# First layer of a two-layer encoder on one core: convolution taps, low halves of weights and the order of the output projection

## The chip, the cores and the metric

The kernel runs on one core of a Trainium2 chip, in one launch. The core has five engines that work side by side, each through its own instructions in order: TensorE (PE; its weight loads, PEld, overlap its matmuls), VectorE (DVE), ScalarE (ACT), GpSimd (POOL) and SyncE (SP, which here issues the DMAs). They wait for each other through semaphores. The metric is the device time of one execution in microseconds (us). The kernel before has a median of 2307.87 us over three runs (2307.01 to 2309.32).

## The reference

The input is 1024 positions by 1024 features, in float32. Layer 0 mixes a convolution branch with a gated branch; layer 1 is differential attention; a squared-ReLU MLP follows each. The change lies in layer 0's mixer, and in how the weights of layer 1 are made ready. Cut to what matters:

```python
def conv_gmlp_mixer(h, w_in, conv_w, conv_b, conv_ln_g, conv_ln_b,
                    sg_ln_g, sg_ln_b, sg_w, sg_b, w_out):
    z = h @ w_in                              # 1024 -> 512 value, 512 gate, 1024 for gMLP
    a = z[..., :512] * sigmoid(z[..., 512:1024])
    a = depthwise_conv(a, conv_w, width=31, centred) + conv_b
    a = silu(layernorm(a, conv_ln_g, conv_ln_b))
    zs = gelu(z[..., 1024:])
    u = zs[..., :512]
    v = layernorm(zs[..., 512:], sg_ln_g, sg_ln_b)
    v = einsum('gpq,bnqgc->bnpgc', sg_w, v.reshape(B, 8, 128, 4, 128)) + sg_b
    return concatenate([a, u * v], axis=-1) @ w_out

# per layer: x = x + gate * mixer(modulate(rmsnorm(x), shift, scale))
#            x = x + gate' * (relu(h' @ w1) ** 2 @ w2),  h' = modulate(rmsnorm(x), ...)
# (shift, scale, gate) = split(silu(c) @ mod_w + mod_b, 3)
```

## The kernel before

**Matmuls.** Activations lie with features on the partitions, in tiles of 128 by 512 positions (two column halves, `c` = 0 and 1). A float32 product is made of three matmuls in a faster format: each operand is split into a high half, rounded to that format, and a low half, the remainder. `mm3` issues high·high (L130), high·low (L131) and low·high (L132).

**Weights.** `prep` (L105 to L114) loads a 128x1024 piece into `raw` (SP issues the load), ScalarE casts it to `whi` (L112), and VectorE subtracts to give `wlo` (L113); in attention the subtraction is POOL's (`eng`). `raw`, `whi` and `wlo` rotate over three buffers each. 61 weights go this way: 4 stripes `wg` and 4 pieces `wa` for the gated linear unit, 8 stripes `wv` for the gMLP values (the four are loaded once for each `c`), 4 pieces `wa` for `u`, 9 pieces of `wo` for layer 0's output projection, then 24 of `wqkv` and 8 of `wo` in layer 1. The MLP weights have a path of their own and are not touched.

**Layer 0 in the order of the code.** The gated linear unit fills four padded tiles `ap`, one for each 128 channels. The values `vg` (gelu, eight tiles of 128 positions by 512) follow, and their LayerNorm is applied by VectorE (L504, `tensor_scalar` with mean and 1/deviation). For each of four groups, `u` is projected, then `gating` multiplies `vg` by the position weights (L522, 128x128 matmuls), VectorE scales and shifts the result into `tt` (L525) and multiplies it into `u` (L529); the first three groups gate after the third `u`, the last after the fourth. `split` makes the pair `zh` (ScalarE, L254) and `zl` (VectorE, L255) for the projection.

**The convolution** runs meanwhile, channel tile by channel tile (`i` = 0 to 3). 20 of 31 taps are VectorE's, summed in PSUM (`ca`, one buffer; L593, L595). For the other 11, ScalarE makes the products (the first one straight into `a1`, L587; the others into `pr`, two buffers, L590) and POOL adds them to `a1` (L591, ten adds for each channel tile). L596 adds `ca` and `a1` into a third tile, `a0`. The names in the trace are `a` for `a0` and `a1`.

**The convolution's LayerNorm** runs for each column half over the four channel tiles: matmuls with ones give the mean (L607), VectorE subtracts it (L611), ScalarE squares (L613), matmuls give the variance (L614), `rstd_of` makes 1/deviation (L198 and L207 to L213), VectorE multiplies (L625), ScalarE takes the sigmoid (L627), VectorE applies gain and bias (L628) and multiplies by the sigmoid (L630), and `split` makes `zh` and `zl`.

**The output projection** has two halves: `project_half(1, c, i)` uses the gated branch, `project_half(0, c, i)` the convolution branch. Each adds `gate` times its result to `x` (`upd`, L278). The modulation vectors (shift, scale, gate) come from `mod_unit`: a load of 512 KB into `mraw` (two buffers) and a multiply with sum on VectorE (L147). `queue_mod` queues them; `bg` and `tick` let them out.

**What sets the order.** A scheduler orders the instructions on each engine from the order of the code, buffers and dependencies; `high_priority` puts the LayerNorm statistics ahead. Pools rotate: "mm" has six PSUM banks, "cv" six tiles of 128x1024.

Of the kernel before, what the change touches and what calls it, by code (L numbers as in the profile page):

```python
# [10 lines left out]
F32 = mybir.dt.float32  # L11
# [7 lines left out]
P = 128  # L19
# [11 lines left out]
SUB_EPS = 1e-5  # L31
TAPS = 31
PAD = TAPS // 2
DVE_TAPS = 20
B_BUFS = 8

V_MIXG, V_MLPG, V_FING = 0, 16, 32
# [10 lines left out]
def trunk(ctx: ExitStack, tc: tile.TileContext, t_in, out):  # L48
# [3 lines left out]
    def f32(ap):  # L52
        return ap.bitcast(F32)
# [53 lines left out]
    def prep(src, own=None, eng=None):  # L107
        raw = wp.tile([P, D], F32, name="raw", tag="raw", bufs=3)
        load(raw, src)
        hi = (own or wp).tile([P, D], F32R, name="whi", tag="whi", bufs=1 if own else 3)  # L110
        lo = (own or wp).tile([P, D], F32R, name="wlo", tag="wlo", bufs=1 if own else 3)
        act.copy(out=hi, in_=raw)  # L112
        (eng or dve).tensor_tensor(out=lo, in0=raw, in1=f32(hi), op=ALU.subtract)  # L113
        return hi, lo  # L114

    class Stream:
# [55 lines left out]
    def vcol(v):  # L172
        return vec[:, v:v + 1]
# [173 lines left out]
    with opened(name="mix", bufs=1) as mp, ExitStack() as pst:  # L347
# [152 lines left out]
        dve.tensor_tensor(out=vt, in0=vr, in1=vr, op=ALU.mult)  # L500
        dve.tensor_tensor(out=vt, in0=vt, in1=vv, op=ALU.mult)
        dve.scalar_tensor_tensor(out=vr, in0=vt, scalar=1.5, in1=vr, op0=ALU.add, op1=ALU.mult)
        for t in range(8):
            dve.tensor_scalar(out=vg[t], in0=vg[t], scalar1=mv[:, t, 0:1], scalar2=vr[:, t:t + 1],  # L504
                              op0=ALU.subtract, op1=ALU.mult)


        ps = bank()
# [56 lines left out]
        def project_half(half, c, i):  # L565
            w = wu.get(4 + 4 * (1 - half) + i)
            for m in (2 * (i % 4), 2 * (i % 4) + 1):
# [6 lines left out]
                if half == 0:  # L574
                    nrm.add(c, x[m][c])


        acc = []
        for i in range(4):
            a = padded[i]  # L580
            a0 = mp.tile([P, T], F32, name="a0", tag="cv", bufs=6)
            a1 = mp.tile([P, T], F32, name="a1", tag="cv", bufs=6)

            def cw(w):
                return vcol(V_CW + w * 4 + i)

            act.activation(out=a1, in_=a[:, DVE_TAPS:DVE_TAPS + T], func=AF.Copy, scale=cw(DVE_TAPS))  # L587
            for w in range(DVE_TAPS + 1, TAPS):
                pr = mp.tile([P, T], F32, name="pr", tag="pr", bufs=2)
                act.activation(out=pr, in_=a[:, w:w + T], func=AF.Copy, scale=cw(w))  # L590
                conv_end = pool.tensor_tensor(out=a1, in0=a1, in1=pr, op=ALU.add)  # L591
            ca = cvps.tile([P, T], F32, name="ca", tag="ca")
            dve.tensor_scalar(out=ca, in0=a[:, 0:T], scalar1=cw(0), scalar2=vcol(V_CB + i), op0=ALU.mult, op1=ALU.add)  # L593
            for w in range(1, DVE_TAPS):
                dve.scalar_tensor_tensor(out=ca, in0=a[:, w:w + T], scalar=cw(w), in1=ca, op0=ALU.mult, op1=ALU.add)  # L595
            dve.tensor_tensor(out=a0, in0=ca, in1=a1, op=ALU.add)  # L596
            acc.append(a0)

        rs = []
        for c in range(NC):
# [10 lines left out]
                    act.activation(out=sq, in_=y, func=AF.Square)  # L613
                    last = pe.matmul(pvar, ones, sq, start=i == 0, stop=i == 3)  # L614
            rs.append(rstd_of(pvar, 512, eps_l, after=last if c == 0 else None))
        queue_mod(0, [16])
        bg(100)
        queue_mod(1, [8, 0], conv_end)
        queue_mod(1, [16])
        bg(18)  # L620
        for c in range(NC):
            cs = slice(c * C, (c + 1) * C)
            for i in range(4):
# [1 line left out]
                dve.tensor_tensor(out=y, in0=y, in1=rs[c], op=ALU.mult)  # L625
                sg = tmp.tile([P, C], F32, name="sg", tag="ht", bufs=3)
                act.activation(out=sg, in_=y, func=AF.Sigmoid, scale=vcol(V_CLG + i), bias=vcol(V_CLB + i))  # L627
                dve.tensor_scalar(out=y, in0=y, scalar1=vcol(V_CLG + i), scalar2=vcol(V_CLB + i),  # L628
                                  op0=ALU.mult, op1=ALU.add)
                dve.tensor_tensor(out=y, in0=y, in1=sg, op=ALU.mult)  # L630
                z[i][c] = htile()
                split(*z[i][c], y)
        for i in range(4):
            for c in range(NC):
                project_half(1, c, i)

        h = [[None] * NC for _ in range(KT)]
        for c, seq in ((0, (0, 1, 2, 3)), (1, (3, 2, 1, 4))):
# [575 lines left out]
```

## Time and profile before

| what | value |
|---|---|
| median of three runs | 2307.87 us (2307.01 to 2309.32) |
| the profiled execution's own time | 2309.78 us |
| its span in the trace | 2308.0 us |
| its mean granted TensorE clock | 0.982 |
| ScalarE busy | 1175.9 us (51%) |
| POOL busy | 205.3 us (9%) |
| DMA, mean over the span | 145 GB/s |

Each row of a group gives the line in the kernel, the engine, the operation, output and input by their names, shapes and count; then busy us and the mean ns of one; then the engine's idle time just before such instructions, with what ended it. A row of the timeline gives the start, the duration and the instruction, and in brackets the idle time before it and what released it. A row of the windows gives the stretch, its length, busy us and instructions of PE, PEld, DVE, ACT and POOL, then the granted TensorE clock, the DMA share and GB/s. Layer 0's mixer takes roughly the first 350 us.

### The profile page before, as it was taken

To read this page: it belongs to the slowest core of one execution; us is meant where nothing else is said; L and a number is where in the kernel's file an instruction comes from. 1 tells how busy PE (TensorE), PEld (TensorE's weight loads), DVE (VectorE), ACT (ScalarE), POOL (GpSimd) and SP (SyncE) were. 2 spreads that over 40 slices of the span, in tenths; PEclk is the share of its full clock that TensorE was granted. 3 is DMA by queue.
4 is the path that set the end of the run, shared out by engine and by line. 5 is a ranking of instruction groups with operands and counts; after the bars stand their busy time and mean duration, and the time that the engine had idled before them with its cause. 6 is when DMAs were issued, how large, how long until landed. Compare 5 with 4: busy or idle time off the path is not lost. (4 is left out here: it accounts for less than half of the span.)

```text
span 2308.0 us, 27492 instructions
## 1 busy us (share of the span) xinstructions
PE 2193.2 (95%) x10144; PEld 1802.1 (78%) x10144; DVE 1872.2 (81%) x2599; ACT 1175.9 (51%) x1745; POOL 205.3 (9%) x109
## 2 busy tenths in 40 slices
PE   4997599999999999989999999999999999999997
PEld 3786387778888888868888888887778888888886
DVE  8899899997795976987878888876699659578497
ACT  4554246643534535445666666654366354353455
POOL 0484000000000000001111111110000000000002
PEclk9998799999999999999999999999999999999999
DMA  8221553837547267234545333361352461643712
GB/s 320 83 74 46 191 159 136 326 110 275 190 155 280 102 223 261 87 110 98 100 86 109 77 84 72 81 202 51 116 228 107 163 229 47 211 144 110 246 46 74
DMA packets 113863, 335.17 MB, mean 145 GB/s; under 512 B 20576, under 2 KB 23520, under 8 KB 112704
## 3 DMA queue, kind: packets, MB, share of 16 engines
q1 hardware_dynamic: 113728, 333.41, 44.7%
q8 instruction: 80, 1.31, 0.2%
q14 instruction: 55, 0.45, 0.1%
HBM read 279.79 MB, written 53.58 MB: 144 GB/s over the span
## 5 line engine op out<-in xcount | busy, mean ns | idle before, releaser
L131 PE MATMUL ps<-b,whi 128*128 128x512 f32 (+1 forms) x1808 | 701.3, 389 | 5.6 <-DVE b L255 5.6
L130 PE MATMUL ps<-b,whi 128*128 128x512 f32 (+1 forms) x1808 | 693.7, 390 | 5.8 <-ACT b L254 3.9
L132 PE MATMUL ps<-b,wlo 128*128 128x512 f32 (+1 forms) x1808 | 693.9, 389 | 1.6 <-DVE wlo L255 1.6
L254 ACT CAST whi<-raw 128x1024 fp32r<-128x1024 f32 (+1 forms) x225 | 236.5, 1051 | 355.1 <-PE ps L131 317.3
L130 PEld LDWEIGHTS ps<-b,whi 128*128 128x128 f32 x1808 | 341.3, 189 | 78.9 <-ACT b L254 5.1
L131 PEld LDWEIGHTS ps<-b,whi 128*128 128x128 f32 x1808 | 341.1, 189 | 77.9 <-DVE b L255 7.5
L132 PEld LDWEIGHTS ps<-b,wlo 128*128 128x128 f32 x1808 | 340.9, 189 | 72.1 <-DVE wlo L255 2.1
L255 DVE TENSOR_TENSOR wlo<-raw,whi 128x1024 fp32r<-128x1024 f32 (+1 forms) x225 | 274.1, 1218 | 139.4 <-ACT whi L254 137.2
L130 PE MATMUL ps<-hh,whi 128*128 128x512 f32 x576 | 225.7, 405 | 32.7 <-ACT hh L249 15.7
L131 PE MATMUL ps<-hl,whi 128*128 128x512 f32 x576 | 229.8, 399 | 6.6 <-DVE hl L250 6.6
L132 PE MATMUL ps<-hh,wlo 128*128 128x512 f32 x576 | 228.4, 397 | 0.0
L743 DVE SCALAR_TENSOR_TENSOR x<-ps,mod,x 128x512 f32<-128x512 f32 x220 | 159.8, 746 | 41.5 <-PE ps L132 41.1
L962 ACT ACTIVATE L<-L,mn 128x1024 f32<-128x1024 f32 x128 | 147.1, 1150 | 90.8 <-DVE mn L960 89.4
L960 DVE CUSTOM_DVE_ANT_0 L<-S,B 128x1024 f32<-128x1024 f32 x128 | 156.0, 1223 | 34.7 <-PE pt L982 17.4
L113 POOL TENSOR_TENSOR wlo<-raw,whi 128x1024 fp32r<-128x1024 f32 x24 | 64.4, 2683 | 1181.6 <-PE S L957 808.4
L130 PEld LDWEIGHTS ps<-hh,whi 128*128 128x128 f32 x576 | 110.1, 192 | 60.9 <-ACT hh L249 20.1
L254 ACT CAST b<-f 128x512 fp32r<-128x512 f32 x192 | 118.0, 619 | 76.5 <-PE ps L132 74.8
L255 DVE TENSOR_TENSOR b<-f,b 128x512 fp32r<-128x512 f32 x192 | 128.9, 684 | 10.2 <-ACT b L254 10.2
L131 PEld LDWEIGHTS ps<-hl,whi 128*128 128x128 f32 x576 | 110.6, 192 | 32.7 <-DVE hl L250 10.1
L132 PEld LDWEIGHTS ps<-hh,wlo 128*128 128x128 f32 x576 | 110.4, 192 | 24.1 <-issue 0.5
L147 DVE CUSTOM_DVE_ANT_0 mraw<-mraw,cact 128x1024 f32<-128x1024 f32 x96 | 116.2, 1218 | 6.9 <-DMA mraw<-in_modw 6.8
L732 ACT COPY f<-ps 128x512 f32<-128x512 f32 x96 | 56.1, 588 | 126.8 <-PE ps L132 126.7
(195 smaller groups left out, 3463.6 us busy)
## 6 DMA issues: line engine op xcount, KB each, us to landing
b<-tspl SPq DMA_DIRECT2D x168, 512.0 KB, 5.3
raw<-in_wm SPq DMA_DIRECT2D x128, 512.0 KB, 4.6
mraw<-in_modw SPq DMA_DIRECT2D x96, 512.0 KB, 4.5
tspl<-b SPq DMA_DIRECT2D x56, 512.0 KB, 4.3
raw<-in_wqkv SPq DMA_DIRECT2D x24, 512.0 KB, 4.8
raw<-in_wo SPq DMA_DIRECT2D x17, 512.0 KB, 3.5
x<-in_xT SPq DMA_DIRECT2D x32, 256.0 KB, 5.8
tsr<-tsp SPq DMA_DIRECT2D x8, 1024.0 KB, 7.7
```

The lines of the kernel that those rows point to most:

```text
L113: (eng or dve).tensor_tensor(out=lo, in0=raw, in1=f32(hi), op=ALU.subtract)
L130: pe.matmul(ps, wh, ah, start=first, stop=False, skip_group_check=resumed)
L131: pe.matmul(ps, wh, al, start=False, stop=False, skip_group_check=resumed)
L132: newest[0] = pe.matmul(ps, wl, ah, start=False, stop=last, skip_group_check=resumed)
L147: i = dve.tensor_tensor_reduce(out=raw, in0=raw, in1=cact, op0=ALU.mult, op1=ALU.add, scale=1.0, scalar=0.0, accum_out=acc)
L254: act.copy(out=out_h, in_=src)
L255: (lo_eng or dve).tensor_tensor(out=out_l, in0=src, in1=f32(out_h), op=ALU.subtract)
L732: act.copy(out={"X1": c11, "Y1": c22, "X2": c12}[p], in_=ps)
L743: dve.scalar_tensor_tensor(out=x[m][c], in0=ps, scalar=gate(d, m), in1=x[m][c], op0=ALU.mult, op1=ALU.add)
L960: dve.tensor_tensor_reduce(out=L, in0=S, in1=win, op0=ALU.add, op1=ALU.min, scale=1.0, scalar=3e38, accum_out=mn)
L962: act.activation(out=L, in_=L, func=AF.Exp, bias=mn, scale=-1.0, accum_out=s[:, j:j + 1])
```

## The change

1. `DVE_TAPS` goes from 20 to 18: 13 taps are ScalarE's and POOL's, 12 adds for each channel tile.
2. In `prep`, the low half is made by ScalarE writing −`whi` into `wlo`, and a DMA on POOL's queue that reads the weight from DRAM once more and adds it into `wlo`. This holds for all 61 weights, so VectorE's 37 and POOL's 24 subtractions go.
3. The LayerNorm of `vg` is applied by ScalarE (scale and bias per position), with one more small VectorE operation for the bias.
4. The gated half of the output projection, with the modulation units it needs, stands ahead of the convolution in the code, and its loops run over `i` first.
5. The sum of `ca` and `a1` goes back into `a1`; `a0` is dropped.
6. Gain and bias of the convolution's LayerNorm are applied by ScalarE.
7. `bg(18)` stands after that LayerNorm's loop.

```diff
-DVE_TAPS = 20
+DVE_TAPS = 18
...
         act.copy(out=hi, in_=raw)
-        (eng or dve).tensor_tensor(out=lo, in0=raw, in1=f32(hi), op=ALU.subtract)
+        act.activation(out=lo, in_=f32(hi), func=AF.Copy, scale=-1.0)
+        pool.dma_start(out=lo, in_=src, accum_op=ALU.add)
         return hi, lo
...
         dve.scalar_tensor_tensor(out=vr, in0=vt, scalar=1.5, in1=vr, op0=ALU.add, op1=ALU.mult)
+        dve.scalar_tensor_tensor(out=vt, in0=mv[:, :, 0], scalar=-1.0, in1=vr, op0=ALU.mult, op1=ALU.mult)
         for t in range(8):
-            dve.tensor_scalar(out=vg[t], in0=vg[t], scalar1=mv[:, t, 0:1], scalar2=vr[:, t:t + 1],
-                              op0=ALU.subtract, op1=ALU.mult)
+            act.activation(out=vg[t], in_=vg[t], func=AF.Identity, scale=vr[:, t:t + 1], bias=vt[:, t:t + 1])
...
+        queue_mod(0, [16])
+        bg(100)
+        for i in range(4):
+            for c in range(NC):
+                project_half(1, c, i)
         acc = []
         for i in range(4):
             a = padded[i]
-            a0 = mp.tile([P, T], F32, name="a0", tag="cv", bufs=6)
             a1 = mp.tile([P, T], F32, name="a1", tag="cv", bufs=6)
...
-            dve.tensor_tensor(out=a0, in0=ca, in1=a1, op=ALU.add)
-            acc.append(a0)
+            dve.tensor_tensor(out=a1, in0=ca, in1=a1, op=ALU.add)
+            acc.append(a1)
...
             rs.append(rstd_of(pvar, 512, eps_l, after=last if c == 0 else None))
-        queue_mod(0, [16])
-        bg(100)
         queue_mod(1, [8, 0], conv_end)
         queue_mod(1, [16])
-        bg(18)
         for c in range(NC):
...
-                dve.tensor_scalar(out=y, in0=y, scalar1=vcol(V_CLG + i), scalar2=vcol(V_CLB + i),
-                                  op0=ALU.mult, op1=ALU.add)
+                act.activation(out=y, in_=y, func=AF.Identity, scale=vcol(V_CLG + i), bias=vcol(V_CLB + i))
                 dve.tensor_tensor(out=y, in0=y, in1=sg, op=ALU.mult)
                 z[i][c] = htile()
                 split(*z[i][c], y)
-        for i in range(4):
-            for c in range(NC):
-                project_half(1, c, i)
+        bg(18)
```

Three places show how the instructions move. Lines after the change are numbered a little higher (L591 is L597, L607 is L612, L614 is L619, L596 is L602, L525 is L526).

POOL's order before, from its first add to attention (`a_1614`, `a_1669`, `a_1724`, `a_1779` are the sums `a1` of the four channel tiles; L113 is attention's subtraction):

```order
L591 ISA
L591 TENSOR_TENSOR a_1614<-a_1614,pr 128x1024 x10
L591 TENSOR_TENSOR a_1669<-a_1669,pr 128x1024 x10
L591 TENSOR_TENSOR a_1724<-a_1724,pr 128x1024 x10
L591 TENSOR_TENSOR a_1779<-a_1779,pr 128x1024 x10
L113 TENSOR_TENSOR wlo<-raw,whi 128x1024 x5
```

POOL's order after, from its first add to the third channel tile (`a_1913`, `a_1971` and `a_2029` are the sums of the first three; L114 is the adding DMA):

```order
L597 TENSOR_TENSOR a_1913<-a_1913,pr 128x1024 x10
L114 DMA wlo<-in_wa 128x1024
L597 TENSOR_TENSOR a_1913<-a_1913,pr 128x1024 x2
L114 DMA wlo<-in_wv 128x1024
L597 TENSOR_TENSOR a_1971<-a_1971,pr 128x1024 x5
L114 DMA wlo<-in_wv 128x1024
L597 TENSOR_TENSOR a_1971<-a_1971,pr 128x1024 x2
L114 DMA wlo<-in_wv 128x1024
L597 TENSOR_TENSOR a_1971<-a_1971,pr 128x1024
L114 DMA wlo<-in_wv 128x1024
L597 TENSOR_TENSOR a_1971<-a_1971,pr 128x1024 x3
```

The adds, which stood in four unbroken blocks, now alternate with the DMAs: seven DMAs stand before the first add, fifteen between the first and the last of the 48 adds, and all others behind. Each DMA waits for ScalarE's negation.

TensorE's order before, after the fourth group's `u` (`a_1613`, `a_1668`, `a_1723`, `a_1778` are the four sums `a0`, `sgw` the position weights, `zh` and `zl` the gated branch):

```order
L522 MATMUL ps<-sgw,vg 128x128 x5
L607 MATMUL ps<-a_1613,ones_r 128x512
L607 MATMUL ps<-a_1668,ones_r 128x512
L607 MATMUL ps<-a_1723,ones_r 128x512
L522 MATMUL ps<-sgw,vg 128x128 x3
L607 MATMUL ps<-a_1778,ones_r 128x512
L614 MATMUL ps<-sq,ones_r 128x512
L607 MATMUL ps<-a_1613,ones_r 128x512
L607 MATMUL ps<-a_1668,ones_r 128x512
L607 MATMUL ps<-a_1723,ones_r 128x512
L607 MATMUL ps<-a_1778,ones_r 128x512
L614 MATMUL ps<-sq,ones_r 128x512 x4
```

TensorE's order after, 173 matmuls into the gated half of the projection (which begins right behind the last L523, gating's eight 128x128 matmuls):

```order
L131 MATMUL ps<-zh,whi 128x512
L612 MATMUL ps<-a_1913,ones_r 128x512
L612 MATMUL ps<-a_1971,ones_r 128x512
L612 MATMUL ps<-a_2029,ones_r 128x512
L612 MATMUL ps<-a_2087,ones_r 128x512
L132 MATMUL ps<-zl,whi 128x512
L133 MATMUL ps<-zh,wlo 128x512
```

Before, the projection's gated half began behind the statistics' first thirteen matmuls. Now it comes first, and the statistics' first four stand after 174 of its 192 matmuls; the other twelve stand behind 11 more, and the conv half of the projection follows them.

VectorE's order after, at the end of the fourth channel tile (`a_2087` is its sum, whose last add is POOL's; `u`, `tt`, `zl` belong to gating):

```order
L530 TENSOR_TENSOR u<-u,tt 128x512
L256 TENSOR_TENSOR zl<-u,zh 128x512
L602 TENSOR_TENSOR a_2087<-ca,a_2087 128x1024
L526 SCALAR_TENSOR_TENSOR tt<-ps,vec,sgb 128x512
L148 ISA mraw,mod<-mraw,cact 128x1024
L148 ISA mod 128x1
L526 SCALAR_TENSOR_TENSOR tt<-ps,vec,sgb 128x512
```

and the place of that sum before (`a_1778`, behind all of gating; L611 subtracts the mean):

```order
L595 SCALAR_TENSOR_TENSOR ca<-ap,vec,ca 128x1024
L157 TENSOR_TENSOR mod<-mod,vec 128x8
L595 SCALAR_TENSOR_TENSOR ca<-ap,vec,ca 128x1024 x2
L596 TENSOR_TENSOR a_1778<-ca,a_1779 128x1024
L611 SCALAR_TENSOR_TENSOR a_1613<-ps,a_1613 128x512
L611 SCALAR_TENSOR_TENSOR a_1668<-ps,a_1668 128x512
```

The final sum stood behind all of gating with the statistics right after it; it now stands ahead of the last group's two `tt`, and the statistics come later.

## The prediction

> **What bounds the kernel now.** First the page's head, for the bounding engine; then the waits of that engine up to 330 us, where the changed code runs; then its windows there.
>
> ```profile
> span 2308.0 us, 27492 instructions
> PE 2193.2 (95%) x10144; PEld 1802.1 (78%) x10144; DVE 1872.2 (81%) x2599; ACT 1175.9 (51%) x1745; POOL 205.3 (9%) x109
> PE ps L607 <- DVE a L596: 23.1, 1, 23.1
> PE ps L130 <- DVE tt L525: 15.0, 1, 15.0
> PE ps L237 <- DVE ss L233: 14.9, 2, 13.8
> PE ps L130 <- ACT hh L249: 12.9, 4, 8.0
> PE ps L614 <- ACT sq L613: 2.8, 2, 1.4
> 210.00:232.00 22.00, 6.46 (x40) 5.78 (x41) 21.58 (x19) 2.84 (x3) 7.89 (x4) 0.68 0.16 50
> 232.00:262.00 30.00, 15.77 (x66) 12.01 (x64) 30.00 (x42) 7.66 (x12) 2.76 (x1) 0.78 0.41 124
> 262.00:288.00 26.00, 14.28 (x27) 5.98 (x28) 18.65 (x28) 5.00 (x7) 0.00 (x0) 0.66 0.78 280
> 300.00:330.00 30.00, 30.00 (x134) 24.86 (x133) 30.00 (x51) 14.62 (x18) 0.00 (x0) 1.00 0.55 175
> ```
>
> TensorE is busy 95% of the span, so time comes back only where it stands idle or slow. Waits are total, times, longest. The first, second and fifth (41 us) lie in the convolution stretch. There VectorE is full (windows: length, then PE, PEld, DVE, ACT and POOL busy, clock, DMA share, GB/s: DVE 21.58 of 22, 30.00 of 30) and TensorE's clock is 0.66 to 0.78; in 300–330 it is 1.00, and a matmul comes every 30.00/134 = 0.224 us. The gate projection ahead also feels VectorE, through L237 and L249. So what feeds TensorE here and leans on VectorE is what the change can win.
>
> TensorE's timeline gives the marks (start, duration, then the idle time before):
>
> ```profile
> 210.52 4.06 PE L522 MATMUL ps<-sgw,vg 128*128 128x128 f32 x34 [0.70 <-DVE vg L504]
> 229.60 0.79 PE L130 MATMUL ps<-hh,whi 128*128 128x512 f32 x1 [15.03 <-DVE tt L525]
> ...
> 270.89 2.08 PE L607 MATMUL ps<-a,ones_r 128*128 128x512 f32 x2 [23.12 <-DVE a L596]
> ...
> 286.17 0.79 PE L130 MATMUL ps<-zh,whi 128*128 128x512 f32 x1
> ```
>
> Gating starts at 210.5, waits 15.0 for `tt` behind taps, then 23.1 for the last convolution channel. The gating half of the output projection (192 matmuls, 43.2 us at 0.225) starts at 286.2 and covers the rest of the convolution's LayerNorm. The conv half then starts near 286.2 + 43.2 + 2.8 (three statistics products inside it at some 0.9, an estimate) = **332.2**. I work out where it starts after.
>
> **The change part by part.**
>
> ```profile
> L591 POOL TENSOR_TENSOR a<-a,pr 128x1024 f32<-128x1024 f32 x40 | 104.4, 2610 | 132.7 <-ACT pr L590 103.8 <-ACT a L587 26.3
> L595 DVE SCALAR_TENSOR_TENSOR ca<-ap,vec,ca 128x1024 f32<-128x1024 f32 x76 | 97.5, 1283 | 1.5
> L147 DVE CUSTOM_DVE_ANT_0 mraw<-mraw,cact 128x1024 f32<-128x1024 f32 x40 | 48.5, 1218 | 6.9 <-DMA mraw<-in_modw 6.8
> L590 ACT ACTIVATE pr<-ap,vec 128x1024 f32<-128x1024 f32 x40 | 45.9, 1153 | 35.3 <-POOL a L591 35.3
> L113 DVE TENSOR_TENSOR wlo<-raw,whi 128x1024 fp32r<-128x1024 f32 x28 | 42.8, 1530 | 2.5 <-ACT whi L112 2.5
> L112 ACT CAST whi<-raw 128x1024 fp32r<-128x1024 f32 x28 | 29.2, 1044 | 16.5 <-PE ps L131 11.7 <-PE ps L132 2.7 <-DMA raw<-in_wg 2.1
> L504 DVE TENSOR_SCALAR vg<-vg,mv,vr 128x512 f32<-128x512 f32 x8 | 16.3, 2111 | 0.0
> L278 DVE SCALAR_TENSOR_TENSOR x<-ps,mod,x 128x512 f32<-128x512 f32 x20 | 14.9, 749 | 0.0
> L628 DVE TENSOR_SCALAR a<-a,vec 128x512 f32<-128x512 f32 x8 | 4.1, 544 | 0.0
> 87.16 25.68 POOL L591 TENSOR_TENSOR a<-a,pr 128x1024 f32<-128x1024 f32 x10 [85.82 <-ACT pr L590]
> ...
> 199.92 10.26 POOL L591 TENSOR_TENSOR a<-a,pr 128x1024 f32<-128x1024 f32 x4 [0.35 <-ACT pr L590]
> ...
> 235.69 2.76 POOL L591 TENSOR_TENSOR a<-a,pr 128x1024 f32<-128x1024 f32 x1 [17.03 <-ACT pr L590]
> raw<-in_wa SPq DMA_DIRECT2D x8, 512.0 KB, 3.5
> raw<-in_wv SPq DMA_DIRECT2D x8, 512.0 KB, 3.6
> 8.33 0.33 SPq L87 DMA_DIRECT2D raw<-in_wg  x1
> DMA to landing us min/median/max: 3.3/7.3/10.2
> L113 POOL TENSOR_TENSOR wlo<-raw,whi 128x1024 fp32r<-128x1024 f32 x24 | 64.4, 2683 | 1181.6 <-PE S L957 808.4
> 194.13 16.33 DVE L504 TENSOR_SCALAR vg<-vg,mv,vr 128x512 f32<-128x512 f32 x8
> 173.00:210.00 37.00, 36.82 (x168) 30.23 (x166) 36.29 (x37) 21.47 (x27) 19.26 (x8) 1.00 0.15 43
> ```
>
> (Groups: count, busy us, mean ns, then idle time before. DMA issues: KB, median us to landing. The landing range is that of `raw` up to 90 us.) VectorE sheds 28 low halves (42.8), eight normalisations (16.3), eight affines (4.1) and eight taps (8 × 1.283 = 10.3): 73.5 us up to 346. ScalarE gains 28 negations (29.2 at a cast's 1.044), eight products (8 × 1.153 = 9.2) and sixteen row operations; in 173–210 it was busy 21.47 of 37, beside TensorE's 36.82, so I cost these at nothing except where a chain passes through them; without that cover they could cost up to their sum. POOL gains eight adds (8 × 2.61 = 20.9) and the adding DMAs.
>
> Two prices no row shows. **POOL's time for one adding DMA**: from 0.33, what SP needs to issue a load of this size, to 2.68, POOL's own whole-tile subtract. I take 1.2: it is an issue, so nearer to SP's row, but POOL is slow (its subtract takes 2.68 where VectorE's takes 1.53) and the DMA also waits in order for ScalarE's negation. **Its landing**: from 3.5, a plain load here, to 2 × 10.2 = 20.4, two slow ones. I take 7, two reads of 3.6, since the addition reads weight and tile. The Trainium skill, "DMA: Bandwidth & Descriptors", section "Anatomy of one DMA — SWDGE (gpsimd) path", fits 2.0 us plus bytes/436e3, an estimate of 3.2 us here; by it the forecast would fall some 4 us, and no run shows it yet.
>
> ```profile
> 45.00:50.00 5.00, 4.62 (x11) 3.13 (x11) 5.00 (x12) 0.89 (x2) 0.00 (x0) 0.50 1.02 407
> ```
>
> *Start.* Here the DMA engines are full at 407 GB/s. Some three adding reads (1.57 MB) fall before the first gate stripes are multiplied; they cost 3.9 us, 7.7 if reading the tile counts too; four subtracts fewer give VectorE 4.9. I take +3, bounds −4 and +8.
>
> *gMLP values.* Each weight stripe feeds 24 matmuls, 5.4 us. From the second adding DMA to the last, POOL has six DMAs and eleven adds in order: 6 × 1.2 + 11 × 2.61 = 35.9, against 6 × 5.4 = 32.4 for TensorE. That is +3.5, and about 4 once for the longer way cast, negation, issue, landing: I take +8. Bounds −2 (all hidden) to +28 (second rival). Gating then starts at 210.5 + 3 + 8 = 221.5. The normalisations go from 16.3 on VectorE to ScalarE, beside TensorE's last stripe but one.
>
> The Trainium skill, "SBUF — State Buffer", section "Who interferes with whom", has a VectorE tensor_scalar in a two-port mode and GpSimd lock each other out, also from writing descriptors. The trace agrees for the compute side: L504 took 2111 ns at 194 to 210, beside POOL's adds, L628 544 ns at the same size with POOL at 0.00.
>
> *POOL's end, E.* It begins at 87.2 + 4, does 48 adds (125.3), fifteen DMAs between them (18), and waits some 3: E = 237.5, about as before (235.7 + 2.76 = 238.5). The two stops for a free buffer (26.3 on L587) go, since a sum needs one buffer less. New are the waits of the DMAs for ScalarE, with the adds queued behind them on POOL, and behind POOL's last add the final sum and gating's last two `tt` on VectorE.
>
> *Gating to statistics.* From 221.5: 24 small matmuls 2.9 (4.06/34 each), the fourth `u` 10.8, eight small 1.0, 18 of the projection 4.1, so 240.3. The next needs the fourth group's `z`. On VectorE that stands behind the last channel's final sum, which needs POOL's last add: 1.2 for the sum, two `tt`, `u`, a modulation and `zl` make it E + 6.3 = **243.8**. Then 156 matmuls at 0.225 (35.1): the mean matmuls run at 278.9. The waits of 15.0 and 23.1 and the slow clock go; 3.5 us of wait is left.
>
> *LayerNorm tail.* It loses its cover: the conv half of the projection now waits for it.
>
> ```profile
> 313.17 0.68 DVE L255 TENSOR_TENSOR zl<-a,zh 128x512 fp32r<-128x512 f32 x1
> ```
>
> From the mean matmul at 270.89 to this first `zl` it took 43.0 us. Between those two VectorE now has eight modulations instead of twelve (−4.9), one `x` update instead of six (−3.7), no affine (−1.1, +0.7 on ScalarE) and no subtract (−1.2): 32.8 us, and the first conv matmul needs only `zh`, 1.3 earlier: 31.5. Bounds: 25, if the modulations are ready each time, and 41.7, if their loads set the pace (VectorE waited 6.9 on them). The conv half starts at 278.9 + 31.5 = **310.4**, 21.8 earlier.
>
> *Elsewhere.*
>
> ```profile
> 1200.00:1400.00 200.00, 199.45 (x1104) 169.97 (x1103) 162.96 (x269) 123.77 (x196) 32.17 (x15) 1.00 0.40 89
> ```
>
> In attention TensorE runs 199.45 of 200, so what hides there is hidden by it. POOL's 24 subtracts of 2.68 become DMAs; ScalarE gains 24 × 1.04 = 25 us beside its 123.77 of 200, bounds 0 and 25; I take 1. In the last projection one stripe's low half (1.05 + 1.05 + 1.2 + 7 = 10.3) has only a stripe's cover (5.4): 2 of up to 5. Together +3.
>
> Sum: −21.8 + 3 = −18.8 on the profiled execution's 2309.8, so 2291.0. Its time lies 1.9 above the median of the runs: **2289**.
>
> **The rivals.**
>
> 1. *POOL becomes the bound: slower.* POOL works in order, and E + 72.9 is the conv half's start. Each microsecond on the fifteen DMAs costs 15. Even is at 332.2 − 3 = 329.2, that is 1.2 + 18.8/15 = 2.45 us for each, waits at its head included; 3.5 gives 2289 + 34.5 = 2323. For it: ScalarE's negation and its products stand in one order, and the products already wait 35.3 for POOL. Against: 2.45 is nearly POOL's whole-tile arithmetic. By the skill's lock-out above, `tensor_scalar` would also hold up descriptors, but L504 and L628 leave VectorE.
> 2. *Low halves land late.* At 12 instead of 7, cast, negation, issue, a queue of 3 and landing take 18; over two stripes ahead 9, against 5.4: eight stripes cost 29. Gating starts at 242.5, the mean matmuls run at 242.5 + 14.7 + 39.2 = 296.4, the conv half starts at 327.9: 2307, no change. For it: `raw` took up to 10.2. Against: the DMA share in 210–232 is 0.16.
> 3. *Nothing new waits.* DMA issues at 0.5 and short landings: gating at 213, mean matmuls at 268.4, a tail of 26: 294.4, with +1 elsewhere 2271. For it: TensorE had no wait on a low half up to 330 us.
> 4. *The tail does not shrink*, its modulations being paced by loads: 41.7 instead of 31.5, 2299.
>
> **How the numbers follow.** Forecast (2277 to 2295) 0.45; third rival 0.12; fourth 0.10; second 0.12; first 0.21. Under 0.2% (4.6 us) a measurement of this kernel can't be told from no change. Faster 0.67, same 0.12, slower 0.21. The range runs from 2266, below the third rival, to 2324, the first with 3.5 us a DMA; beyond that about 0.15 is left. The likeliest case's own range lies on one side, 2277 to 2295.
>
> **What would show it.** Right: TensorE's 15.0 on `tt` and 23.1 on the last channel are gone; a wait of 3 to 6 on `zl` or `zh` of the fourth group near 240, and one near 30 on the conv half's first `zh` after the mean matmuls; gating near 221; POOL's last add ending near 237; adding DMAs landing in about 7. Wrong: waits on `wlo` among the value stripes above 15 in sum (second rival); POOL's last add after 260 (first); a tail above 38 (fourth); new waits of TensorE in attention above 5.

## The result, and the profile after

The changed kernel takes 2324.84 us (median of four runs, 2321.33 to 2325.34); the kernel before took 2307.87 beside it (three runs, 2307.01 to 2309.32; a fourth took 3727.18 and is left out as slow). The ratio is 1.0068 (95% interval 1.0056 to 1.0079): slower by 0.7%. The profiled execution has a span of 2322.6 us, 14.6 more than before.

The page's head of the changed kernel, then four rows of TensorE's waits over the whole span (total, times, longest):

```profile
span 2322.6 us, 27621 instructions
PE 2203.6 (95%) x10144; PEld 1809.1 (78%) x10144; DVE 1799.7 (77%) x2539; ACT 1249.9 (54%) x1827; POOL 208.2 (9%) x154
PE ps L131 <- ACT zh L255: 20.1, 2, 13.1
...
PE ps L131 <- DVE v L1009: 6.0, 1, 6.0
...
PE ps L133 <- DMA wlo<-in_wo: 5.4, 1, 5.4
PE ps L131 <- DMA th<-osp: 5.1, 1, 5.1
```

VectorE is 72 us less busy, and the two old waits (15.0 on `tt`, 23.1 on the last channel) are gone. In their place stand 20.1 on the conv branch's and the gated branch's `zh`, 5.4 on a low half, and two in layer 1 (`v` and `th`).

TensorE's timeline of the changed kernel at the marks of the prediction, and where the first MLP begins:

```profile
244.86 0.80 PE L131 MATMUL ps<-zh,whi 128*128 128x512 f32 x1 [6.99 <-ACT zh L255]
...
284.19 3.60 PE L612 MATMUL ps<-a,ones_r 128*128 128x512 f32 x8
...
322.98 0.79 PE L131 MATMUL ps<-zh,whi 128*128 128x512 f32 x1 [13.07 <-ACT zh L255]
...
349.25 0.80 PE L133 MATMUL ps<-zh,wlo 128*128 128x512 f32 x1 [5.42 <-DMA wlo<-in_wo]
349.85 0.63 PE L131 MATMUL ps<-zh,whi 128*128 128x512 f32 x1
350.27 0.63 PE L132 MATMUL ps<-zl,whi 128*128 128x512 f32 x1
...
355.39 0.42 PE L131 MATMUL ps<-zh,whi 128*128 128x512 f32 x1
...
380.46 0.47 PE L131 MATMUL ps<-b,whi 128*128 128x512 f32 x1 [1.76 <-DVE x L279]
```

The conv half (the convolution's half of the output projection) starts at 323.0; in the kernel before it started near 332. Nine microseconds are won there. But from that mark to the first MLP it takes 57.5 us instead of some 45, so the MLP begins at 380.5, against 377.3 before: 3.2 late. The other 11.4 of the 14.6 are lost behind it.

### The profile page after: what moved, and what is told of

It reads as the page before. It is cut to its first block, busy times and chain, and to the rows that moved or that the text cites. A ratio compares the mean times of both kernels' runs of the same rounds, so it can differ in the third digit from the quotient of the medians.

```text
span 2322.6 us, 27621 instructions
## 1 busy us (share of the span) xinstructions
PE 2203.6 (95%) x10144; PEld 1809.1 (78%) x10144; DVE 1799.7 (77%) x2539; ACT 1249.9 (54%) x1827; POOL 208.2 (9%) x154
## 4 chain that ended last, share of the span: by engine, by line
PE 81%; DVE 8%; DMA 5%; ACT 3%; issue 2%; POOL 1%; DVEq 0%; SPq 0%; POOLq 0%; ACTq 0%
PE ps L131 23%; PE ps L133 23%; PE ps L132 23%; DMA mraw<-in_modw 2%; PE S L955 2%; PE pt L981 2%; PE S L956 2%; PE ps L992 1%; PE ps L993 1%; PE ps L994 1%; DVE mraw L148 1%; DVE wlo L256 1%; DVE b L256 1%; DVE ht L243 1%; POOL a L597 1%
## 5 line engine op out<-in xcount | busy, mean ns | idle before, releaser
L131 PE MATMUL ps<-hh,whi 128*128 128x512 f32 x576 | 232.4, 406 | 16.4 <-ACT hh L250 14.6
L132 PEld LDWEIGHTS ps<-hl,whi 128*128 128x128 f32 x576 | 111.0, 193 | 29.3 <-DVE hl L251 7.0
L148 DVE CUSTOM_DVE_ANT_0 mraw<-mraw,cact 128x1024 f32<-128x1024 f32 x96 | 116.2, 1219 | 19.6 <-DMA mraw<-in_modw 19.6
L597 POOL TENSOR_TENSOR a<-a,pr 128x1024 f32<-128x1024 f32 x48 | 121.2, 2532 | 12.5 <-ACT pr L596 10.2
```

The source lines that it names most:

```text
L131: pe.matmul(ps, wh, ah, start=first, stop=False, skip_group_check=resumed)
L132: pe.matmul(ps, wh, al, start=False, stop=False, skip_group_check=resumed)
L148: i = dve.tensor_tensor_reduce(out=raw, in0=raw, in1=cact, op0=ALU.mult, op1=ALU.add, scale=1.0, scalar=0.0, accum_out=acc)
```

## The experiments

Eighteen other kernels, each with a profile and three rounds, against the kernel before on the same chip. "First MLP" is the first matmul of the first MLP in the trace (layer 0's mixer ends there); "rest" is the span less that.

| kernel | median us | ratio to before, 95% | first MLP | rest |
|---|---|---|---|---|
| before | 2307.87 | 1 | 377.3 | 1930.7 |
| changed | 2324.84 | 1.0068 (1.0056–1.0079) | 380.5 | 1942.1 |
| e1 | 2308.94 | 1.0004 (0.9991–1.0017) | 381.1 | 1924.9 |
| e2 | 2312.04 | 1.0017 (1.0004–1.0031) | 373.6 | 1939.0 |
| e3 | 2305.62 | 0.9988 (0.9975–1.0000) | 373.9 | 1928.7 |
| e4 | 2304.83 | 0.9980 (0.9971–0.9990) | 361.5 | 1942.6 |
| e5 | 2297.49 | 0.9954 (0.9940–0.9969) | 360.6 | 1934.5 |
| e6 | 2279.94 | 0.9877 (0.9862–0.9892) | 344.0 | 1934.9 |
| e7 | 2309.39 | 1.0011 (0.9998–1.0024) | 381.0 | 1928.7 |
| e8 | 2293.00 | 0.9934 (0.9917–0.9950) | 362.9 | 1928.9 |
| e9 | 2307.25 | 0.9994 (0.9985–1.0004) | 376.4 | 1933.2 |
| e10 | 2296.41 | 0.9947 (0.9932–0.9961) | 364.9 | 1929.2 |
| e11 | 2315.99 | 1.0032 (1.0020–1.0044) | 384.7 | 1929.6 |
| e12 | 2287.72 | 0.9908 (0.9891–0.9924) | 346.0 | 1942.7 |
| e13 | 2290.05 | 0.9922 (0.9896–0.9948) | 342.9 | 1941.8 |
| e14 | 2321.21 | 1.0059 (1.0039–1.0079) | 345.8 | 1972.7 |
| e15 | 2277.53 | 0.9872 (0.9846–0.9899) | 347.9 | 1932.6 |
| e16 | 2295.85 | 0.9952 (0.9935–0.9968) | 368.4 | 1925.3 |
| e18 | 2295.39 | 0.9943 (0.9924–0.9963) | 363.9 | 1930.1 |
| e20 | 2282.57 | 0.9888 (0.9874–0.9903) | 347.0 | 1931.4 |

### Where the adding DMAs help and where they cost (e1 to e5)

In e1 (layer 1), e2 (layer 0) and e3 (everywhere) the changed kernel has its low halves subtracted again; e4 is the kernel before with nothing but the adding DMAs, e5 with those of layer 0 alone. The edit of e1; e2 turns the condition round, and e5 makes the same choice in the kernel before (`layer1` is filled where layer 1's weights begin):

```diff
-        act.activation(out=lo, in_=f32(hi), func=AF.Copy, scale=-1.0)
-        pool.dma_start(out=lo, in_=src, accum_op=ALU.add)
+        if layer1:
+            (eng or dve).tensor_tensor(out=lo, in0=raw, in1=f32(hi), op=ALU.subtract)
+        else:
+            act.activation(out=lo, in_=f32(hi), func=AF.Copy, scale=-1.0)
+            pool.dma_start(out=lo, in_=src, accum_op=ALU.add)
```

> The changed kernel, with layer 1's 32 low halves (wqkv, wo) subtracted as before; layer 0 keeps its adding DMAs. Theory A (the adding DMAs' traffic costs 11.4 us behind the first MLP's start, where the changed kernel was 3.2 us late, by late loads at 1550 and 1634): about 2313 us, those two waits gone. Theory B (the 11.4 us come from a shifted order alone, whatever makes the low halves): 2322 to 2326.

> The changed kernel, with layer 0's 29 low halves subtracted on VectorE as before; layer 1 keeps its adding DMAs. Theory A (in layer 0 the adding DMAs crowd the modulation and x loads, DMA share 0.99 at 250 to 260, and hold the mean's subtraction back to 293.9): the first conv matmul 8 to 12 us earlier than 323.0, the 5.4 us wait on wo's low half gone, 2308 to 2316. Theory O (the statistics behind the projection leave the LayerNorm's tail bare in any case, and VectorE's 29 subtractions cost what the loads gain): first conv matmul near 320 or later, 2320 to 2328.

> The changed kernel without any adding DMA (all 61 low halves subtracted as before): taps, order and ScalarE's LayerNorm work alone. Theory A: both savings, 2296 to 2304. Theory O: layer 1's 11.4 back but none in layer 0, 2311 to 2316.

> The kernel before with all 61 low halves by adding DMAs and nothing else changed. Theory A: layer 1's loss of 8 to 12 us shows here too, 2314 to 2322 with layer 0 within 5. Theory B: 2306 to 2311.

> The kernel before, with adding DMAs for layer 0's 29 low halves alone and layer 1 subtracted as before. If the old order gains 15.8 us up to the first MLP from the adding DMAs (361.5 against 377.3) and layer 1's DMAs lose it again (about 12): 2292 to 2296. If the gain of layer 0 hangs on something later and is lost again in any case: 2303 to 2309.

In layer 1 the cost that theory A named is there: the three kernels that add in the whole of it have a rest of 1939.0 to 1942.6; with subtraction it lies between 1924.9 and 1934.9 in the table (e14 aside). Its size is not one number: adding in layer 1 costs 15.9 us by the medians in the changed order (changed against e1), 6.4 where layer 0 subtracts (e2 against e3) and 7.3 in the old order (e4 against e5). No run shows why these differ. e1 came 4 below the 2313 that A had.

In layer 0 theory A misses its own mark. TensorE's timeline of e2 has the first conv matmul here:

```profile
326.61 2.93 PE L136 MATMUL ps<-zh,whi 128*128 128x512 f32 x6 [11.99 <-ACT zh L260]
```

That is 3.6 us later than the changed kernel's 323.0 (e3: 326.6), where A had it 8 to 12 earlier and theory O near 320 or later. The stretch that the prediction calls the tail, from the mean matmuls to this mark, takes 35.2 us instead of 38.8, while VectorE's waits for modulation loads up to 346 us fall from 19.6 to 11.4: taken together with the subtractions that e2 gives back to VectorE, the adding DMAs lengthen the tail by some 4 us and no more. The MLP still starts 7 us earlier without adding DMAs (373.6, 373.9), and what is won lies behind the mark: e2's conv half takes 47.0 us instead of 57.5, without the wait on the low half. e2's time lies in A's range for all that; e3 came out at 2305.6, 1.6 above A's range and 5 below O's.

In the old order the same DMAs bring the first MLP 16 us forward (377.3 to 361.5), which is why e4, at 2304.8, lies below both of its ranges: A had allowed 5 for layer 0. So layer 0's adding DMAs are good in the old order, layer 1's are bad, and something else in the change eats what layer 0's bring. e5 has the one without the other: 2297.5, 1.5 above the first range given.

### The parts of layer 0, one at a time (e6, e7, e8, e18)

On top of e5: e6 adds ScalarE's two LayerNorm moves (parts 3 and 6), e7 the reordering (parts 4, 5 and 7), e8 the 18 taps. e18 is the kernel before with only parts 3 and 6. The edits are pieces of the diff shown above; e6's:

```diff
+        dve.scalar_tensor_tensor(out=vt, in0=mv[:, :, 0], scalar=-1.0, in1=vr, op0=ALU.mult, op1=ALU.mult)
         for t in range(8):
-            dve.tensor_scalar(out=vg[t], in0=vg[t], scalar1=mv[:, t, 0:1], scalar2=vr[:, t:t + 1],
-                              op0=ALU.subtract, op1=ALU.mult)
+            act.activation(out=vg[t], in_=vg[t], func=AF.Identity, scale=vr[:, t:t + 1], bias=vt[:, t:t + 1])
...
-                dve.tensor_scalar(out=y, in0=y, scalar1=vcol(V_CLG + i), scalar2=vcol(V_CLB + i),
-                                  op0=ALU.mult, op1=ALU.add)
+                act.activation(out=y, in_=y, func=AF.Identity, scale=vcol(V_CLG + i), bias=vcol(V_CLB + i))
```

> The kernel before with layer 0's adding DMAs, and the normalisation of vg and the affine of the convolution's LayerNorm on ScalarE. If VectorE bounds the stretch (tt waited 11.2 us there): 8 to 16 us less than the kernel without these two moves, 2278 to 2286. If ScalarE's eight row operations stand in gating's way instead: within 3 of it or above.

> The kernel before with layer 0's adding DMAs, and the gating half of the projection ahead of the convolution in the code (with a0 dropped, bg(18) moved, loops i before c): the reordering alone. Theory O (the reordering leaves the LayerNorm's tail bare and holds VectorE's mean subtraction behind modulations): first MLP 12 to 20 us later than without it (361.5), 2304 to 2314. If taps or ScalarE's work were what costs: within 4 of it, 2291 to 2298.

> The kernel before with layer 0's adding DMAs and 18 instead of 20 taps on VectorE: the taps alone. If VectorE bounds (8 taps of 1.283 less, 10.3): 4 to 10 us less than with 20 taps. If POOL's eight adds (20.9 us) decide: 5 to 15 more, since its last add then ends behind VectorE's last tap.

> The kernel before with only the two LayerNorm moves to ScalarE, no adding DMA. If adding DMAs and ScalarE's work each take their share of VectorE (each gained 10 to 18 us on top of the other): 2290 to 2298. If one of them alone is enough: 2278 to 2283.

From e5's 360.6 the first MLP moves to 344.0 with ScalarE's moves, to 381.0 with the reordering, to 362.9 with the taps. The reordering alone costs 20.4 us there, a little over the 12 to 20 of theory O, whose range in time holds. The taps alone can't be told from none. e6, in its first range, is 1.2% below the kernel before; only e15 and e20 below come as near, and within noise can't be told from it. e18, inside its range, shows that the two savings on VectorE add, and a little more (13.4 and 16.7 against 33.3 for both).

### Reordering and taps together (e9, e16, e10, e20)

All four have layer 0's adding DMAs, ScalarE's moves, and layer 1 subtracted. e9 has 18 taps in the old order, e16 the reordering with 20 taps; e10 (18 taps) and e20 (20) put only half of the gating projection ahead:

```diff
-        for i in range(4):
+        for i in range(2):
             for c in range(NC):
                 project_half(1, c, i)
...
         bg(18)
+        for i in range(2, 4):
+            for c in range(NC):
+                project_half(1, c, i)
```

> The changed kernel with the reordering undone and layer 1's low halves subtracted as before: adding DMAs in layer 0, 18 taps and ScalarE's LayerNorm work together. If the reordering cancels what the others gain: 2274 to 2283, first MLP near 344 instead of 381. If the taps' POOL adds take the place of VectorE as the bound: 2284 to 2292, with TensorE waiting over 10 us for the last channel's sum.

> The changed kernel with layer 1 subtracted as before (2308.9 us) and only half of the gating projection ahead of the convolution; the other half behind the LayerNorm's loop in the code. Theory of cover (the statistics' PSUM bank comes free only when the projection is nearly done, and nothing is left to cover the tail): mean matmuls near 262 instead of 287, 96 matmuls (21.6 us) as cover, first MLP 10 to 20 us earlier, 2289 to 2299. Theory of pacing (VectorE's modulations alone set the tail): under 6 us earlier, 2303 or more.

> The changed kernel with layer 1 subtracted as before (2308.9 us) and 20 instead of 18 taps on VectorE, the reordering kept: POOL has eight adds less. Without the reordering these eight adds cost 27 us (2279.9 against 2307.3). If the reordering holds the first MLP back whatever POOL does: within 5 of 2308.9, first MLP near 378 to 382. If POOL's late last add is what the reordered kernel pays for: 2290 to 2300.

> The changed kernel with layer 1 subtracted as before, only half of the gating projection ahead (2296.4 us with 18 taps), and 20 taps on VectorE. If the cover is back and POOL's adds were the rest: 2276 to 2286, as the old order gives. If VectorE's eight taps (10.3 us) then bound: 2296 to 2304.

| median us | old order | half ahead | all ahead |
|---|---|---|---|
| 20 taps on VectorE | 2279.94 (e6) | 2282.57 (e20) | 2295.85 (e16) |
| 18 taps | 2307.25 (e9) | 2296.41 (e10) | 2308.94 (e1) |

e10, e16 and e20 came inside the ranges of the theories of cover and of POOL's late adds. e9 missed both of its ranges, and by more than any price I had. The row of TensorE's timeline with its long wait in e9; VectorE's waits on POOL for the sum of a channel (total, times, longest; the list begins behind the first such wait, of 8.6 us); and two of these sums in VectorE's timeline, the third channel tile's and the last:

```profile
264.33 1.22 PE L613 MATMUL ps<-a,ones_r 128*128 128x512 f32 x1 [29.91 <-DVE a L602]
```

```profile
DVE a L602 <- POOL a L597: 12.4, 1, 12.4
```

```profile
203.81 1.23 DVE L602 TENSOR_TENSOR a<-ca,a 128x1024 f32<-128x1024 f32 x1 [12.36 <-POOL a L597]
263.05 1.23 DVE L602 TENSOR_TENSOR a<-ca,a 128x1024 f32<-128x1024 f32 x1
```

POOL's last add in e9, then in e6:

```profile
241.53 2.49 POOL L597 TENSOR_TENSOR a<-a,pr 128x1024 f32<-128x1024 f32 x1
```

```profile
212.48 2.66 POOL L597 TENSOR_TENSOR a<-a,pr 128x1024 f32<-128x1024 f32 x1
```

POOL's last add ends at 244.0 in e9, at 215.1 in e6, which has eight adds less. But POOL does not hold the kernel at its end: e9's last sum comes 19 us after it, without a wait. It holds VectorE earlier, channel by channel. `ca` is one buffer, so the next channel's taps can't start before the sum of the last one has read it, and that sum waits for POOL: 20.9 us in two waits between 80 and 300 us, against 1.4 in e6. ScalarE, which makes POOL's products, waits 25.3 for POOL to give back `pr`, against 14.1, and VectorE 11.5 for ScalarE's `vg`, against 2.7. The four sums start at 113.0, 143.0, 177.5 and 215.2 in e6 and at 119.4, 158.6, 203.8 and 263.1 in e9, later each time, and TensorE waits 29.9 for the last of them. Behind 203.8 VectorE has no idle time left: the last channel's 18 taps stand there among gating and other work in a different order. How much of the 27.3 us is POOL's hold and how much that order was not taken apart. The waits also turn up only beside ScalarE's moves: e8, with the same taps, loses nothing.

The two taps cost 27.3 us in the old order, 13.1 with the reordering and 13.8 with half of it: that the projection put ahead covers part of POOL's lateness fits these numbers. The reordering costs 15.9 with 20 taps and nothing clear with 18. So the full reordering buys back about what it costs when POOL is late, and only costs when POOL is not. Most of that price comes off with half of it: with 18 taps the matmuls for the LayerNorm's mean come at 264.8 in e10 (287 in e1), and 96 matmuls are left to cover the tail.

### What makes the tail long (e11)

e11 is e1 with the first MLP's modulation units queued behind the LayerNorm's last low half:

```diff
-        queue_mod(1, [8, 0], conv_end)
-        queue_mod(1, [16])
...
-                split(*z[i][c], y)
+                last = split(*z[i][c], y)
+        queue_mod(1, [8, 0], last)
+        queue_mod(1, [16])
         bg(18)
```

> The changed kernel with layer 1 subtracted as before (2308.9 us), and the 24 modulation units of the first MLP queued behind the LayerNorm's last low half: VectorE has none ahead of the mean's subtraction and none in the tail. Theory of pacing: the wait for the first conv matmul (14.2 us) shrinks to under 6 and that matmul comes at 300 to 308 instead of 325; the units are then late for the MLP's norm, so the first MLP is 0 to 12 us earlier. Theory of cover: the first conv matmul at 315 or later, the first MLP 5 to 20 us later.

VectorE's group of modulations up to 346 us, in the changed kernel, then TensorE's timeline of e11, from the mean matmuls on:

```profile
L148 DVE CUSTOM_DVE_ANT_0 mraw<-mraw,cact 128x1024 f32<-128x1024 f32 x40 | 48.5, 1220 | 19.6 <-DMA mraw<-in_modw 19.6
```

```profile
285.78 3.60 PE L617 MATMUL ps<-a,ones_r 128*128 128x512 f32 x8
...
309.86 0.80 PE L136 MATMUL ps<-zh,whi 128*128 128x512 f32 x1 [5.87 <-ACT zh L260]
...
380.53 1.22 PE L243 MATMUL ps<-ss,ones_r 128*128 128x512 f32 x1 [11.14 <-DVE ss L239]
```

Without the modulations in its way the first conv matmul comes at 309.9 instead of 325.2 (e1), its wait 5.9 instead of 14.2, a little later than the theory of pacing had it (300 to 308). The tail is 24.1 us, against 38.2 in e1. But the first MLP then waits 11.1 for a norm that stands behind those units: it begins 3.6 us later than e1's, where that theory had it earlier, and the kernel is 7 us slower. So the units do set the tail, and the work is real too: it has to be hidden beside matmuls, and e11 found no place for it in the reordered kernel. In the changed kernel VectorE waits 19.6 us for modulation loads (the group above), against 6.9 before.

### Layer 1 (e12 to e15)

On top of e6: e12 has adding DMAs for wqkv, e13 for wo, e15 only ScalarE's negation (then overwritten by the subtraction), and e14 reads each weight twice without adding:

```diff
         load(raw, src)
+        if layer1:
+            pool.dma_start(out=raw, in_=src)
```

> The fastest kernel so far (2279.9 us: old order, adding DMAs in layer 0, ScalarE's LayerNorm work) with adding DMAs for layer 1's 24 wqkv pieces too, wo subtracted. If the loss in layer 1 is that of the late th loads and Q/K steps beside these reads: 2283 to 2288. If it is that of wo's eight pieces in the last projection: within 2 of 2279.9.

> The fastest kernel (2279.9 us) with adding DMAs for layer 1's eight wo pieces only, wqkv subtracted. If the wo pieces' longer way costs the last projection a wait on the low half (4.9 us where wo was last added, at half clock behind it): 2284 to 2290. If wqkv's pieces carry the whole loss of layer 1: within 2 of 2279.9.

> The fastest kernel (2279.9 us) with each of layer 1's 32 weights read a second time into the same tile by a plain DMA on POOL's queue, and subtracted as before: the traffic and the second landing without the addition, and without ScalarE's negation. Theory of traffic (reads compete with the Q, th and w transfers): 2286 to 2292. Theory of waits in the order (a TensorE bank held for VectorE's v, the chain over ScalarE): within 3 of 2279.9.

> The fastest kernel (2279.9 us) with ScalarE also writing the negated high half of layer 1's 32 weights, which POOL's or VectorE's subtraction then overwrites: ScalarE's 34 us alone. If ScalarE's work is what layer 1 pays for: 2285 to 2292. If it lies beside TensorE's work, as the prediction had it: within 3 of 2279.9.

ScalarE's negations cost nothing (2277.5 against 2279.9), where the prediction took 1. e12 and e13 lose 7.8 and 10.1 by the medians, e12 inside its first range and e13 at the end of its own. The two losses don't add: e4, which has both, loses 7.3 against e5. In both the longest new wait lies in the last projection. TensorE's timeline of e12, of e13 and of the changed kernel there:

```profile
1595.66 0.80 PE L135 MATMUL ps<-th,whi 128*128 128x512 f32 x1 [4.51 <-DVE v L1014]
```

```profile
1619.24 0.80 PE L137 MATMUL ps<-th,wlo 128*128 128x512 f32 x1 [5.14 <-DMA wlo<-in_wo]
```

```profile
1634.05 0.79 PE L131 MATMUL ps<-th,whi 128*128 128x512 f32 x1 [5.99 <-DVE v L1009]
```

`v` of the last head waits for a DMA in every kernel (3.9 to 11 us); what differs is whether TensorE waits for `v`. In e12, e4 and the changed kernel it does, for 4.5, 7.0 and 6.0 us; the kernel before and all the others, e2 among them, show no such wait. That the PSUM bank of that matmul is one that `v` still reads is my reading of it; no run shows it, nor why it should be so in these three alone. In e13, and in e2, TensorE waits for wo's low half, whose way is longer than one stripe's cover. The wait on `th` is seen in just the kernels that add wo in layer 1 (changed 5.1, e2 3.4, e4 2.6, e13 3.6). The row of the changed kernel:

```profile
1550.50 0.80 PE L131 MATMUL ps<-th,whi 128*128 128x512 f32 x1 [5.13 <-DMA th<-osp]
```

e14 was to take the traffic by itself and did not: it lost 41 us, far outside both of its ranges, but by another way. Its TensorE waits between 950 and 1720 us begin with

```profile
PE ps L939 <- ACT vT L936: 32.1, 7, 7.9
```

By my reading, ScalarE casts `whi` in order, and with the second landing ahead of the cast the value copies queued behind it came late. What e14 does show is that twice the reads alone bring none of the waits on `th`, `v` or `wlo`. From the last norm matmul ahead of the second MLP to that MLP's first matmul it takes 53.7 us, as the kernel before, e1, e6 and e15 do, against 61.0 in e12, 62.7 in e13 and 63.0 in the changed kernel. Since e14 runs 41 us slower, its reads are also spread differently, so traffic is made unlikely by it and not ruled out.

## Why the prediction was wrong, point by point

The sum foresaw −18.8 for the span, and +14.6 was measured. The steps that failed are the tail (31.5 put down, 38.8 measured), the length of the conv half (put at "as before", 12.4 longer) and the 3 us for everything else (11.4). The 33.4 us between forecast and result are 12.6 at the start of the conv half (5.3 at the mean matmuls, 7.3 in the tail), 12.4 in its length and 8.4 elsewhere. Behind them stands a judgement that the sum never tested: reordering and taps were taken as gains, and the runs show that each costs where the other parts are in place.

- **Start and values.** +3 and +8 were foreseen, gating at 221.5. The value stretch started 2.7 late, and gating, which in the kernel before began at 208.1 ahead of the wait at 210.5, came at 210.4, 2.3 late: the eight for the values did not come. POOL's next add starts 0.61 us after an adding DMA, half of the 1.2 taken. The landing was nearer to the 7 taken: 5.7 us for wv, 10.0 for wqkv. The first row below is of the kernel before, all others of the changed one. The Trainium skill's fit ("DMA: Bandwidth & Descriptors", "Anatomy of one DMA — SWDGE (gpsimd) path") gave an estimate of 3.2 us; the measured times are some two to three times that. Gating's small matmuls were counted as 24 and eight, where the trace has records of 48 and 16: 3.9 us too little, which did not show, because TensorE then waited 7.0 for `z`.

```profile
208.10 1.72 PE L522 MATMUL ps<-sgw,vg 128*128 128x128 f32 x14
```

```profile
210.45 4.62 PE L523 MATMUL ps<-sgw,vg 128*128 128x128 f32 x40
```

```profile
118.61 0.89 POOL L114 DMA_DIRECT2D wlo<-in_wv  x1
119.22 12.68 POOL L597 TENSOR_TENSOR a<-a,pr 128x1024 f32<-128x1024 f32 x5
...
221.38 11.06 POOL L597 TENSOR_TENSOR a<-a,pr 128x1024 f32<-128x1024 f32 x4
...
raw<-in_wqkv SPq DMA_DIRECT2D x24, 512.0 KB, 9.2
wlo<-in_wqkv POOLq DMA_DIRECT2D x24, 512.0 KB, 10.0
...
wlo<-in_wv POOLq DMA_DIRECT2D x8, 512.0 KB, 5.7
```

- **POOL's end** at 237.5: its last four adds, in the row at 221.38 above, end at 232.4, 5 us early. **The fourth group's `z`** at 243.8: TensorE's row at 244.86, shown with the result. The number is right by luck. The path was to be POOL's last add, then the last sum; but the sum, below, has no wait on POOL. VectorE was busy with a low half and modulations when POOL was done, and from POOL's end to `z` it took 12.4 us instead of 6.3.

```profile
236.41 1.21 DVE L602 TENSOR_TENSOR a<-ca,a 128x1024 f32<-128x1024 f32 x1
```

```profile
DVE a L602 <- POOL a L597: 14.5, 2, 8.4
```

  The taps were priced as 10.3 us off VectorE, and POOL's 20.9 us more as harmless, because E was about the old end. That comparison looked at POOL's last add alone. Between 80 and 300 us VectorE waits 14.5 us for POOL at the sums of the first two channel tiles (second row; none in the kernel before), and with eight adds less these waits are 1.5 us and the kernel is 13.1 us faster (e16 against e1).
- **The mean matmuls** at 278.9: they ran at 284.2 (the row at 284.19). Of the 5.3 us, 1.1 are the later `z`. TensorE ran 163 matmuls in between and not 156, and the first of them, behind the wait of 7.0, came 0.43 us apart instead of 0.225.
- **"The conv half starts at 278.9 + 31.5 = 310.4"**: 284.2 + 38.8 = 323.0, 12.6 late. The tail is nearly that of the fourth rival (41.7). I had taken fewer modulations between the marks as time saved, and not asked where the others went: they stand ahead of the mean's subtraction, which came 9.7 us behind its matmul. Two rows of VectorE's timeline show it:

```profile
287.35 1.22 DVE L148 CUSTOM_DVE_ANT_0 mraw<-mraw,cact 128x1024 f32<-128x1024 f32 x1 [3.68 <-DMA mraw<-in_modw]
...
293.87 2.48 DVE L616 SCALAR_TENSOR_TENSOR a<-ps,a 128x512 f32<-128x512 f32 x4
```

  e11 moved exactly these, and its tail is 24.1 us where e1's is 38.2: near the bound of 25 that the prediction gave for modulations that are ready each time. The DMAs were full ahead of these rows (at 250 to 260 the windows below give a share of 0.99), but without the adding DMAs the tail was still 35.2 (e2): they account for some 4 of the 7.3.

```profile
250.00:260.00 10.00, 10.00 (x46) 8.25 (x45) 5.32 (x10) 2.11 (x2) 0.00 (x0) 1.00 0.99 338
300.00:320.00 20.00, 9.10 (x19) 3.07 (x18) 14.84 (x24) 8.80 (x12) 0.24 (x1) 0.84 0.71 200
320.00:340.00 20.00, 17.02 (x64) 13.87 (x65) 16.96 (x30) 17.66 (x27) 0.00 (x0) 0.80 0.23 82
340.00:360.00 20.00, 14.58 (x52) 11.43 (x52) 11.32 (x15) 5.68 (x9) 0.87 (x1) 0.83 0.42 130
```

- **A term that was not in the sum.** The conv half was taken to last as long as before. It lasted 12.4 us longer: 5.4 on wo's low half (2 of "up to 5" had been put down, for the last projection of layer 1 only), 1.8 on `x` ahead of the first MLP (the row at 380.46), and the other 5, by my reading, slow clock. Behind the waits of 13.1 and 5.4 the matmuls came 0.43 us apart instead of 0.225 for some 5 us (349.85 and 350.27 above are two of them), and the granted clock of the last two stretches in the windows is 0.80 and 0.83. The old order had its slow clock beside waits that the sum removed; the new waits bring their own.
- **"Together +3" elsewhere**: +11.4. ScalarE's part was right (0, e15). From the first MLP to the last norm in layer 1 the changed kernel loses 7.6, with the wait of 5.1 on `th` in it; the last projection loses 9.3 where 2 had been put down, with the wait of 6.0 on `v`. No row of before shows either wait. Behind it 5.4 come back; no run was made on that.
- **The rivals.** Slower came with its chance of 0.21, but not through the first rival as priced: each DMA took less than taken, and POOL's last add ended at 232.4, not after 260. POOL does hold the kernel, but by its adds at each channel's sum and not by the DMAs at its end. The tail of 38.8 is nearly the fourth rival's 41.7, and its sign (above 38) came.

By the ratios on the same chip, layer 0's adding DMAs and ScalarE's moves are worth −28.4 us (e6: 0.0123 × 2308); the reordering and the taps together cost 29.3 on top (e1 against e6), and layer 1's adding DMAs 14.8 (changed against e1). These are steps from one kernel to the next, so they must come to the +15.7 of the ratio 1.0068; the sum is no check on them. The price of each part holds for the kernel that it was measured in: the reordering costs 20.4 at the first MLP on top of e5, 15.9 in time on top of e6, and nothing clear beside 18 taps (e9 against e1).

## What to carry to other kernels

Relieving the bound engine is worth only what the next engine in line leaves: look at every hand-over between the two, where a buffer is given back, and not only at when the next engine ends. When work is moved ahead to fill a wait, look for what it used to cover, and for what the in-order engines will run in the gap: here modulations, some of them waiting for loads, stood ahead of the one subtraction that everything waited for. A part that helps in one stage can cost in another, so undo a change part by part before dropping it: of this one, layer 0's adding DMAs and ScalarE's LayerNorm moves make a kernel 1.2% faster than before.

## What the runs showed of the hardware that I had not expected

A normalisation of 128x512 on VectorE took 2111 ns beside POOL's adds, and on ScalarE 804 ns in the same place; a row of ScalarE's group in the changed kernel:

```profile
L506 ACT ACTIVATE vg<-vg,vt,vr 128x512 f32<-128x512 f32 x8 | 5.8, 804 | 1.6 <-DVE vt L504 1.6
```

An adding DMA of 512 KB holds POOL's queue for some 0.6 us (the next add starts 0.61 after it, in the rows at 118.61 and 119.22 above), a quarter of an add. The plain loads of the same weights were slower too: wqkv's `raw` went from 4.8 to 9.2 us to landing in the changed kernel (above), and to 10.2 in e12, while reading it twice without adding left it at 3.8 (e14). No run shows why.
